# Output projection of a hybrid layer in seven block products, with weight sums kept in DRAM

## The chip, the cores and the metric

The kernel runs on one core of one Trainium2 chip. The metric is the device time of one execution in microseconds (us); the runs of the kernel before give 2102.1 us in the median.

## What is computed

One layer: a norm, one input projection, two token mixers side by side (HGRN2 and RG-LRU, 512 wide each), an output projection back to the residual stream, and a SwiGLU FFN. x has 2048 tokens of width 1024, all in float32.

```python
def reference(x, ...):
    h = x
    xn = rms_norm(h, mix_norm_w)
    proj = jnp.einsum('bsd,de->bse', xn, w_in)
    q, f_logit, i_v, g, lru_x, lru_gate = jnp.split(proj, ...)
    o_hg = hgrn2_mix(q, f_logit, i_v, g, lb, hg_norm_w)
    o_lru = rglru_mix(lru_x, lru_gate, ...)
    mixed = jnp.concatenate([o_hg, o_lru], axis=-1)
    h = h + jnp.einsum('bse,ed->bsd', mixed, w_out)
    hn = rms_norm(h, ffn_norm_w)
    gate, up = jnp.split(jnp.einsum('bsd,df->bsf', hn, w_gate_up), 2, axis=-1)
    h = h + jnp.einsum('bsf,fd->bsd', jax.nn.silu(gate) * up, w_down)
    return rms_norm(h, final_norm_w)
```

## The kernel before

**Numbers.** A float32 operand is split into a high part (a cast on ACT) and a low part (a subtraction on DVE), and each product of two operands is three matmuls: high by high, high by low, low by high. A matmul is 128x128 by 128x512.

**Stages.** The tokens come in two halves of 1024, and a half in two pieces c of 512 (four token tiles tt of 128). Mixing goes half by half. It makes the values (pv; `tok_wide` L589 in half 0, `tok_mm` L245 in half 1), then eight steps s of feature units (pa and pb, `feat_mm` L234), for HGRN2 where s is even and for the LRU where it is odd, with the state work in hooks between them, then the gate (pg). The gated HGRN2 output v is turned by PE (tp_o, four transposes a tile) and becomes, scaled and split, half of the operand mx; the LRU output y is the other half. The output projection (tiles poh, L1218 to L1246) has 2 pieces x 2 column halves n x 4 token tiles x 8 k x 3 = 384 matmuls a half. DVE adds x from PSUM into h (L1230), and h goes to DRAM. Behind it `scale_h` (L1202) makes the row factor of the FFN's norm and scales h, and `turn_h` (L1208) turns it (tp_hs) and stores it to hn_d. While half 0 is projected, `norm_steps` (L606) prepares the normed x of half 1 (xk, xn).

The FFN follows by halves: `ffn_up` in 22 quads, each in seven block products on sums of activation blocks (act_a to act_g) and of weights (wgu_a to wgu_g), 84 matmuls a quad; `down_quads` in seven products too; and, for six feature tiles of half 0, `down_plain` (L866) in plain products, one pass for c=0 and one for c=1. In the second of these the steps that load hn of half 1 and make its act operands are handed out one by one (`extra`): b_0 to b_3 are four blocks of hn.

**Weights.** `Stream` (L155) loads a weight tile of 512 KB into one of three raw buffers, casts the high part on ACT (L168) and subtracts on DVE (L169) into slots (whi, wlo), of which there are nine. `ahead` asks for tiles before their use.

**Order.** Within an engine instructions run in the order that the program's scheduler gave them, and wait there for their data; the loads and stores that SP issues also stand in one queue. Data wait in pools: 16 pages, 4 xin tiles, 14 blocks, 4 + 4 banks of PSUM. At the start `warm_up` (L518) runs zero matmuls while the first data come in (19 are written, and the trace has 38 records of them).

Of the kernel before, what the change touches and what calls it, by code (L numbers as in the profile page):

```python
# [18 lines left out]
NU = 4  # L19
# [18 lines left out]
def hybrid_layer(ctx: ExitStack, tc: tile.TileContext, x, x_t, norm_w, cols, w_in, gate_w, w_out, w_gu, w_down, out):  # L38
# [116 lines left out]
    class Stream:  # L155
# [3 lines left out]
        def load(self, line, i):  # L159
            src, nm = self.specs[i]  # L160
            raw = rawt("raw_" + nm)
            line(nc.sync.dma_start(out=raw, in_=src))
            return raw
# [23 lines left out]
    for half in range(2):  # L187
        for s in range(24):
            specs.append((w_in[s], f"in{half}_{s}"))
        for c in range(NC):  # L190
            for s in range(8):
                specs.append((w_out[s], f"o{half}_{c}_{s}"))
    ws = Stream(specs)

# [323 lines left out]
    def warm_up():  # L518
        z = late("warm")
        v.memset(z, 0.0)  # L520
        ps = aux("warm")
        for i in range(19):
            nc.tensor.matmul(ps[:, 0:P], lhsT=z[:, 0:P], rhs=z[:, P : 2 * P], start=True, stop=True)
# [10 lines left out]

    def row_factors(c, rows):
        rs = small.tile([P, 4], F32, tag="ss", name=f"ss_x0_{c}", bufs=8)
# [4 lines left out]
        v.scalar_tensor_tensor(out=rs, in0=sums[0], scalar=EPS, in1=sums[1], op0=ALU.add, op1=ALU.add)  # L541
        nc.gpsimd.tensor_tensor(out=rs, in0=rs, in1=mhalf, op=ALU.pow)
        return rs
# [17 lines left out]
    def row_spread(c, rs):  # L561
        nm = f"x0_{c}"
# [16 lines left out]

    def load_x(half, c, tt, nm):  # L580
        r0 = half * T + c * CW + tt * P
        xs = []
        for n in range(2):
            p = page(f"{nm}_{n}")
            nc.sync.dma_start(out=p, in_=x[r0 : r0 + P, n * CW : (n + 1) * CW])
            xs.append(p)
        return xs
# [18 lines left out]
    def norm_steps(half, c):  # L606
        o = half * T + c * CW
        box = {}

        def stat(tt):  # L610
            nm = f"x{half}_{c}_{tt}"
            if tt == 0:
                box["dg"], box["pbc"] = late(f"dg{half}_{c}"), aux(f"tpb{half}_{c}")
            dg, pbc = box["dg"], box["pbc"]
            rs = rstd_of(load_x(half, c, tt, nm), nm)
            ts = slice(tt * P, (tt + 1) * P)
            v.tensor_scalar(out=dg[:, ts], in0=ident, scalar1=rs, scalar2=None, op0=ALU.mult)
            nc.tensor.matmul(pbc[:, ts], lhsT=ones.broadcast_to([P, P]), rhs=dg[:, ts], start=True, stop=True)

        def apply(k):  # L620
            if k == 0:
                box["xn"] = act_tile(f"xn{half}_{c}")
            p = xin(f"xk{half}_{c}_{k}")
            nc.sync.dma_start(out=p, in_=x_t[k * P : (k + 1) * P, o : o + CW])
            v.scalar_tensor_tensor(
                out=p, in0=p, scalar=par[:, C_NW + k : C_NW + k + 1], in1=box["pbc"], op0=ALU.mult, op1=ALU.mult
# [3 lines left out]
        return box, [lambda tt=tt: stat(tt) for tt in range(TPC)], [lambda k=k: apply(k) for k in range(KT)]  # L630

# [442 lines left out]
    for half in range(2):  # L1079
# [12 lines left out]
        for c in range(NC):  # L1092
# [19 lines left out]
            for tt in range(TPC):  # L1112
                ps = tok_mm(wv, xt[c], tt, f"pv{half}_{c}_{tt}")
                nc.scalar.copy(out=vt[:, tt, :], in_=ps)
                if later:
                    later.pop(0)()
# [28 lines left out]
        for s in range(8):  # L1145
            i = s // 2
            ws.ahead(2)
# [24 lines left out]
        mixes = []  # L1172
        for c in range(NC):
# [9 lines left out]
            mx = act_tile(f"mx{half}_{c}")  # L1183
            for tt in range(TPC):
                transpose_in(mx, tt, 0, vts[c][:, tt, :], f"o{half}_{c}_{tt}", par[:, C_HN : C_HN + 1])
            for u in range(NU):
                split([part(mx, s, 4 + u) for s in range(2)], ys[c][:, u, :])
            mixes.append(mx)


        wffn = wvec(1, f"wffn{half}")
        if half == 0:
            boxes, steps = [], [[], []]
            for c in range(NC):
                nb, stats, applies = norm_steps(1, c)
                boxes.append(nb)
                steps[c] = stats + applies
        else:
            bops[0], steps, last = acts(hn_d[0], "0", False)
        hp = {}  # L1200

        def scale_h(half, g, wffn, hp):  # L1202
            rs = rstd_of(hp[g], f"hs{half}_{g}")
            for n in range(2):
                p = hp[g][n]
                v.scalar_tensor_tensor(out=p, in0=p, scalar=rs, in1=wffn[:, n * CW : (n + 1) * CW], op0=MUL, op1=MUL)

        def turn_h(half, g, hp):  # L1208
            nm = f"hs{half}_{g}"
            for n in range(2):  # L1210
                pt = transposed(g, n, hp[g][n], nm)
                q = late(f"ht{nm}_{n}")
                nc.scalar.copy(out=q.rearrange("p (k t) -> p k t", t=P), in_=pt)
                nc.sync.dma_start(
                    out=hn_d[half][n][:, :, g * P : (g + 1) * P].rearrange("k p t -> p k t"), in_=q.rearrange("p (k t) -> p k t", t=P)
                )

        later, turns = [], []  # L1218
        for c in range(NC):
            todo = len(steps[c])  # L1220
            for n in range(2):
                wo = ws.take(4)
                for tt in range(TPC):
                    g = c * TPC + tt
                    nm = f"h{half}_{g}_{n}"
# [126 lines left out]
```

## Time and profile before

| | us |
|---|---|
| runs (median; lowest to highest) | 2102.1; 2102.0 to 2103.07 |
| the profiled execution | 2103.02 |
| its span in the trace | 2101.3 |
| PE, DVE, ACT busy | 2086.6, 1516.6, 1001.5 |

PE is TensorE's matmul stream, PEld its weight loads, DVE VectorE, ACT ScalarE, POOL GpSimd, SP the queue that issues the transfers. A row of a timeline gives start, duration, engine, line, operation, out<-in, shapes and count, and in brackets the idle time before it and what ended it. A row of a window gives each engine's busy time in it with the number of instructions, then the granted clock of TensorE as a share (PEclk), the busy share of the DMA engines and GB/s. A row of what PE waited for gives us in total, times, and the longest. "x256 | 100.7, 393" in a group is count, busy us and mean ns.

### The profile page before, as it was taken

What the parts mean: (1) busy time and instruction counts of PE and PEld (TensorE: products, weight loads), DVE (VectorE), ACT (ScalarE), POOL (GpSimd) and SP (SyncE); (2) the same over time, 40 slices, a digit from 0 to 9 for tenths busy, and PEclk for the clock granted to TensorE, in tenths of its full rate; (3) what the DMA queues carried; (4) which work ended last, traced back from release to release, by engine and by line L of the source; (5) the groups of instructions that cost most, each with busy time, mean ns of one, the idle gap of its engine ahead of it and who ended that gap; (6) DMA issues with size and microseconds to landing.
All of it is one profiled execution on the core that took longest, in us unless ns stands there. A gap on an engine that the chain in (4) does not pass through costs nothing.

```text
span 2101.3 us, 26188 instructions
## 1 busy us (share of the span) xinstructions
PE 2086.6 (99%) x9682; PEld 1730.6 (82%) x9682; DVE 1516.6 (72%) x2467; ACT 1001.5 (48%) x1671; POOL 61.8 (3%) x111
## 2 busy tenths in 40 slices
PE   9999999999999999999999999999999999999998
PEld 8888888888888887888888888887888888888887
DVE  7778856626888558876676669778767676669787
ACT  7677765536777644433333344335333333344333
POOL 1000000100000000000000000000000000000000
PEclk9999999999999999999999999999999999999999
DMA  7111117831111176432232365345423232266424
GB/s 261 51 41 40 32 41 236 275 120 41 41 41 41 61 249 201 146 130 95 87 120 96 106 250 191 116 144 176 147 89 125 96 103 102 96 232 238 160 81 146
DMA packets 139712, 264.94 MB, mean 126 GB/s; under 512 B 11328, under 2 KB 27712, under 8 KB 139584
## 3 DMA queue, kind: packets, MB, share of 16 engines
q1 hardware_dynamic: 139440, 263.24, 37.3%
q8 instruction: 76, 1.25, 0.3%
q14 instruction: 52, 0.43, 0.1%
q10 hardware_dynamic: 144, 0.03, 0.0%
HBM read 200.04 MB, written 63.18 MB: 125 GB/s over the span
## 4 chain that ended last, share of the span: by engine, by line
PE 94%; DVE 3%; DMA 2%; issue 1%; ACT 0%; DVEq 0%; POOLq 0%; POOL 0%; SPq 0%; ACTq 0%
PE quad_e L756 11%; PE quad_g L756 11%; PE quad_a L756 11%; PE pda L1027 10%; PE pdb L1027 6%; PE quad_f L756 6%; PE pb L241 3%; PE pb L242 3%; PE pa L240 3%; PE pa L241 3%; PE pb L240 3%; PE pa L242 3%; PE poh L252 2%; PE poh L253 2%; PE poh L254 2%; PE pv L600 2%
## 5 line engine op out<-in xcount | busy, mean ns | idle before, releaser
L756 PE MATMUL quad_f<-act_f,wgu_f 128*128 128x512 f32 x528 | 127.4, 390 | 1.7 <-ACT wgu_c L212 1.5
L756 PE MATMUL quad_a<-act_a,wgu_a 128*128 128x512 f32 x528 | 127.6, 390 | 0.0
L756 PE MATMUL quad_g<-act_g,wgu_g 128*128 128x512 f32 x528 | 127.1, 390 | 0.0
L756 PE MATMUL quad_a<-act_b,wgu_b 128*128 128x512 f32 x528 | 127.1, 389 | 0.0
L756 PE MATMUL quad_g<-act_d,wgu_d 128*128 128x512 f32 x528 | 127.0, 390 | 0.0
L756 PE MATMUL quad_e<-act_e,wgu_e 128*128 128x512 f32 x528 | 127.0, 389 | 0.0
L756 PE MATMUL quad_e<-act_c,wgu_c 128*128 128x512 f32 x528 | 126.9, 389 | 0.0
L640 DVE TENSOR_TENSOR u<-u,quad_g 128x512 f32<-128x512 f32 x88 | 60.5, 688 | 80.0 <-PE quad_g L756 80.0
L756 PEld LDWEIGHTS quad_f<-act_f,wgu_f 128*128 128x128 f32 x528 | 99.1, 188 | 22.9 <-ACT act_g L212 1.9
L756 PEld LDWEIGHTS quad_g<-act_d,wgu_d 128*128 128x128 f32 x528 | 99.1, 188 | 20.9 <-DVE u L640 0.4
L756 PEld LDWEIGHTS quad_e<-act_c,wgu_c 128*128 128x128 f32 x528 | 99.1, 188 | 20.6
L756 PEld LDWEIGHTS quad_g<-act_g,wgu_g 128*128 128x128 f32 x528 | 99.0, 188 | 20.7 <-DVE wgu_g L213 0.3
L756 PEld LDWEIGHTS quad_e<-act_e,wgu_e 128*128 128x128 f32 x528 | 99.1, 188 | 20.5
L756 PEld LDWEIGHTS quad_a<-act_b,wgu_b 128*128 128x128 f32 x528 | 99.1, 188 | 20.5
L756 PEld LDWEIGHTS quad_a<-act_a,wgu_a 128*128 128x128 f32 x528 | 99.0, 188 | 20.4
L240 PE MATMUL pa<-xn,whi_in 128*128 128x512 f32 x256 | 101.1, 395 | 0.0
L241 PE MATMUL pb<-xn,wlo_in 128*128 128x512 f32 x256 | 100.7, 393 | 0.0
L242 PE MATMUL pb<-xn,whi_in 128*128 128x512 f32 x256 | 100.4, 392 | 0.0
L242 PE MATMUL pa<-xn,whi_in 128*128 128x512 f32 x256 | 100.4, 392 | 0.0
L241 PE MATMUL pa<-xn,wlo_in 128*128 128x512 f32 x256 | 100.4, 392 | 0.0
L240 PE MATMUL pb<-xn,whi_in 128*128 128x512 f32 x256 | 100.2, 392 | 0.0
L254 PE MATMUL poh<-whi_o,mx 128*128 128x512 f32 x256 | 99.2, 392 | 0.0
(337 smaller groups left out, 4902.3 us busy)
## 6 DMA issues: line engine op xcount, KB each, us to landing
raw<-in_w_gu SPq DMA_DIRECT2D x88, 512.0 KB, 3.9
raw_in<-in_w_in SPq DMA_DIRECT2D x47, 512.0 KB, 3.5
ao_p<-as SPq DMA_DIRECT2D x76, 256.0 KB, 2.7
raw_o<-in_w_out SPq DMA_DIRECT2D x32, 512.0 KB, 4.7
xk<-in_x_t SPq DMA_DIRECT2D x32, 256.0 KB, 5.1
x<-in_x SPq DMA_DIRECT2D x32, 256.0 KB, 5.7
xrh<-in_x SPq DMA_DIRECT2D x32, 256.0 KB, 3.5
h<-h SPq DMA_DIRECT2D x32, 256.0 KB, 3.6
```

Source lines behind the costliest of these rows:

```text
L240: nc.tensor.matmul(ps, lhsT=whi[:, ks], rhs=hi, start=(k == 0), stop=False)
L241: nc.tensor.matmul(ps, lhsT=wlo[:, ks], rhs=hi, start=False, stop=False)
L242: nc.tensor.matmul(ps, lhsT=whi[:, ks], rhs=lo, start=False, stop=(k == KT - 1))
L252: nc.tensor.matmul(ps, lhsT=hi, rhs=whi[:, ks], start=(k == 0), stop=False)
L253: nc.tensor.matmul(ps, lhsT=hi, rhs=wlo[:, ks], start=False, stop=False)
L254: nc.tensor.matmul(ps, lhsT=lo, rhs=whi[:, ks], start=False, stop=(k == KT - 1))
L600: ins = nc.tensor.matmul(banks[tt], lhsT=a, rhs=w, start=(k + i == 0), stop=(k == KT - 1 and i == 2))
L640: (e or v).tensor_tensor(out=out, in0=a, in1=b, op=op)
L756: nc.tensor.matmul(ps, lhsT=w[:, s, ks], rhs=x, start=first and k + n == 0, stop=k == 3 and n == 2, skip_group_check=not first)
L1027: nc.tensor.matmul(ps, lhsT=x, rhs=y, start=first and q + n == 0, stop=q == gr.n - 1 and n == 2, skip_group_check=not first)
```

## The change

The projection of a half is taken as one 2x2 product of blocks. The rows are c=0 and c=1, the inner dimension is hg (the turned HGRN2 output) and y, the columns are n=0 and n=1. Seven products replace eight: p1 = hg0 b11, p2 = y0 b21, and five on sums of operands, weights or both. They run in the order of OORDER; two groups of four banks, pox and poy, collect them, so that p6 is added on top of p1, p7 on top of that, and so on, and after each product DVE adds its bank into the right tile of the residual (res, L1303; 28 adds a half, where there were 16). Each product has 4 token tiles x 4 k x 3 = 48 matmuls, and two weight tiles of 512 KB from a stream of its own (wos).

The weight sums for p4, p5, p6 and p7 are made once, in half 0, at s = 1, 3, 5, 7 (`out_sums`): four loads of 256 KB into two of the raw buffers, four subtractions on DVE, four stores to DRAM (wo_p). Both halves load them from there.

The operand sums (`sum_`, L1224) are eight operations of 128x1024 on DVE a half; hg is copied out of PSUM by ACT alone, and splits are 128x1024 (two of them an operand).

h is stored to DRAM, and loaded again where it is scaled and turned (`h_steps`): for half 0 in the pv stage of half 1, for half 1 in the first `ffn_up`, one tile every 14 steps. `norm_steps` takes the squares of x in xin tiles, one power a piece c in place of one a tile, and DVE reads the row of factors from a copy in SBUF. `warm_up` has 11 zero matmuls. In `down_plain` of half 0 two empty steps stand after the first four of `extra`.

```diff
+    OORDER = ("p1", "p2", "p6", "p5", "p7", "p3", "p4")
+    t_d = {name: dram.tile([P, 4, CW], F32, name="wo_" + name) for name in ("p4", "p5", "p6", "p7")}
+    ospecs = []
+    for half in range(2):
+        for name in OORDER:
+            for kp in range(2):
+                at0 = {"p1": 0, "p2": 2, "p3": 6}.get(name)
+                ospecs.append((t_d[name][:, 2 * kp : 2 * kp + 2, :] if at0 is None else w_out[at0 + kp], f"o{half}_{name}_{kp}"))
+    wos = Stream(ospecs)
...
+    def out_sums(k):
+        kp, ks = k // 2, slice((k % 2) * CW, (k % 2 + 1) * CW)
+        r = [rawt(f"wt{u}_{k}") for u in range(2)]
+        for u in range(2):
+            for n in range(2):
+                nc.sync.dma_start(out=r[u][:, n * CW : (n + 1) * CW], in_=w_out[4 * n + 2 * u + kp][:, ks])
+        b11, b12, b21, b22 = (r[u][:, n * CW : (n + 1) * CW] for u in range(2) for n in range(2))
+        v.tensor_tensor(out=b11, in0=b12, in1=b11, op=ALU.subtract)
+        v.tensor_tensor(out=b12, in0=b22, in1=b12, op=ALU.subtract)
+        v.tensor_tensor(out=b22, in0=b22, in1=b11, op=ALU.subtract)
+        v.tensor_tensor(out=b21, in0=b21, in1=b22, op=ALU.subtract)
+        for name, p in (("p5", b11), ("p7", b12), ("p4", b21), ("p6", b22)):
+            nc.sync.dma_start(out=t_d[name][:, k, :], in_=p)
...
-        for i in range(19):
+        for i in range(11):
...
+            pbc = row_spread(c, box["rs"], "x1")
+            box["row"] = late(f"row1_{c}")
+            nc.scalar.copy(out=box["row"], in_=pbc)
...
+            if half == 0 and s % 2:
+                out_sums(i)
...
+        def operand(name, p):
+            op[name] = [block(f"mx_{LET[name]}{s}_{half}") for s in range(2)]
+            for j in (0, 2):
+                split([t[:, j : j + 2, :] for t in op[name]], p[:, j : j + 2, :])
+
+        def sum_(out, a, b, alu):
+            for j in (0, 2):
+                v.tensor_tensor(out=out[:, j : j + 2, :], in0=a[:, j : j + 2, :], in1=b[:, j : j + 2, :], op=alu)
+
...
+                tp = transposed(tt, 0, vts[c][:, tt, :], f"o{half}_{c}_{tt}")
+                nc.scalar.activation(
+                    out=t[:, :, tt * P : (tt + 1) * P], in_=tp, func=AF.Copy, scale=par[:, C_HN : C_HN + 1]
                 )
...
+        def prepare(name):
+            if name == "p6":
+                s1 = part_sums["s1"] = block(f"s1_{half}", F32)
+                s2 = part_sums["s2"] = block(f"s2_{half}", F32)
+                sum_(s1, hg[1], ys[1], ALU.add)
+                sum_(s2, s1, hg[0], ALU.subtract)
+                operand(name, s2)
+            elif name == "p5":
+                operand(name, part_sums["s1"])
+                sum_(hg[1], hg[0], hg[1], ALU.subtract)
+                sum_(ys[0], ys[0], part_sums["s2"], ALU.subtract)
+            elif name == "p7":
+                operand(name, hg[1])
+            elif name == "p3":
+                operand(name, ys[0])
+            elif name == "p4":
+                operand(name, ys[1])
...
+        to = dict(p1=(0, 0), p2=(0, 0), p6=(0, 1), p5=(1, 1), p7=(1, 1), p3=(0, 1), p4=(1, 0))
...
+        for i, name in enumerate(OORDER):
+            wo = wos.take(2)
+            if i < 6:
+                wos.ahead(2)
+                prepare(OORDER[i + 1])
+            if name in ("p2", "p5"):
+                banks_y = [aux(f"poy{name}_{tt}_{half}") for tt in range(TPC)]
+            banks = banks_y if name in ("p2", "p5", "p3") else banks_x
+            first = name in ("p1", "p2", "p5")
+            a = op.pop(name)
+            c, n = to[name]
+            if i in (1, 2, 5):
+                residual_in(*to[OORDER[i + 1]])
+            for tt in range(TPC):
+                tsl, ps = slice(tt * P, (tt + 1) * P), banks[tt]
+                for q in range(4):
+                    whi, wlo = (w[:, (q % 2) * CW : (q % 2 + 1) * CW] for w in wo[q // 2])
+                    ahi, alo = (z[:, q, tsl] for z in a)
+                    for m, (x_, y_) in enumerate(((ahi, whi), (ahi, wlo), (alo, whi))):
+                        nc.tensor.matmul(
+                            ps, lhsT=x_, rhs=y_, start=first and q + m == 0, stop=q == 3 and m == 2, skip_group_check=not first
+                        )
+                g = c * TPC + tt
+                p = res[g, n]
+                v.tensor_tensor(out=p, in0=p, in1=ps, op=ALU.add)
+                if name in ("p2", "p7", "p3", "p4"):
+                    nc.sync.dma_start(out=h_d[half][g][n], in_=p)
+                slot(4 * i + tt)
...
+        def h_steps(g, half=half, ffn_row=ffn_row):
+            ps = []
+            nm = f"hs{half}_{g}"
+
+            def scale():
+                if not ffn_row:
+                    ffn_row.append(wvec(1, f"wffn{half}"))
+                for n in range(2):
+                    p = page(f"{nm}_{n}")
+                    nc.sync.dma_start(out=p, in_=h_d[half][g][n])
+                    ps.append(p)
+                rs = rstd_of(ps, nm)
+                for n in range(2):
+                    v.scalar_tensor_tensor(
+                        out=ps[n], in0=ps[n], scalar=rs, in1=ffn_row[0][:, n * CW : (n + 1) * CW], op0=MUL, op1=MUL
+                    )
+
+            def turn():
...
+            later = [lambda i=i, p=pairs: (p[i][0]() if i < NTT else 0, p[i - 1][1]() if i else 0) for i in range(NTT + 1)]
+        else:
+            idle = [lambda: None]
+            later = idle * 14 + [f_ for p in pairs for f_ in idle + [p[0]] + idle * 2 + [p[1]] + idle * 9]
...
-            extra = steps + last
+            extra = [steps.pop(0) for _ in range(4)] + [lambda: None] * 2 + steps + last
```

**DVE in the output projection of half 0.** Before, around the first residual adds (poh is the projection's bank, ss_x and dg belong to the norm of half 1's x, mx is the operand):

```order
L169 TENSOR_TENSOR wlo_o_0_3_3002<-raw_o_0_3_2999,whi_o_0_3_3001 128x1024
L213 TENSOR_TENSOR mx_1_11_2942<-y_1_681,mx_1_01_2940 128x512 x4
L216 SCALAR_TENSOR_TENSOR mx_1_10_2941<-tp_o_1_3_0_2964,par,mx_1_00_2939 128x4x128
L1230 TENSOR_TENSOR h_0_0_3032<-xrh_0_0_3005,poh_0_0_3007 128x512
L1230 TENSOR_TENSOR h_1_0_3090<-xrh_1_0_3063,poh_1_0_3065 128x512
L206 SCALAR_TENSOR_TENSOR ss_x_0_0_3041<-ss_x_0_0_3041 128x1
L617 TENSOR_SCALAR dg_0_3035<-ident,ss_x_0_0_3041 128x128
L206 SCALAR_TENSOR_TENSOR ss_x_0_1_3054<-ss_x_0_1_3054 128x1
L1230 TENSOR_TENSOR h_2_0_3133<-xrh_2_0_3106,poh_2_0_3108 128x512
L617 TENSOR_SCALAR dg_0_3035<-ident,ss_x_0_1_3054 128x128
```

After, from the last add of p1 (pox) past the first low parts of p6's operand (mx_f); s_0_3172 is the sum s2, each sum being two such rows, and poyp_0_0 is p2's bank of the first token tile:

```order
L1303 TENSOR_TENSOR res_3_0_3048<-res_3_0_3048,pox_0_3053 128x512
L1224 TENSOR_TENSOR s_0_3172<-s_0_3171,hg_0_2839 128x1024
L1224 TENSOR_TENSOR hg_1_3017<-hg_0_2839,hg_1_3017 128x1024
L1303 TENSOR_TENSOR res_0_0_3042<-res_0_0_3042,poyp_0_0_3183 128x512
L1224 TENSOR_TENSOR y_0_676<-y_0_676,s_0_3172 128x1024
L170 TENSOR_TENSOR wlo_o_p_1_3168<-raw_o_p_1_3165,whi_o_p_1_3167 128x1024
L234 TENSOR_TENSOR mx_f_0_3178<-s_0_3172,mx_f_0_3177 128x1024
L1303 TENSOR_TENSOR res_1_0_3044<-res_1_0_3044,poyp_1_0_3184 128x512
```

Behind p1 and p2 now stand the operations on 128x1024 that make the sums, and mx_f comes behind them; before, the adds had row factors and weight low parts between them, and the operand was complete ahead of the first add.

**DVE where the plain down product goes from c=0 to c=1.** Before, the last rows up to the first add that frees a bank (hd from pd):

```order
L213 TENSOR_TENSOR act_d_1_11713<-b_2_1_11860,act_d_1_11712 128x512
L640 TENSOR_TENSOR b_3_1_11941<-b_3_1_11943,b_3_1_11941 128x512
L213 TENSOR_TENSOR ad_1_16_12004<-ad_1_16_12002,ad_1_16_12004 128x512
L213 TENSOR_TENSOR act_e_1_11703<-b_3_1_11940,act_e_1_11702 128x512
L213 TENSOR_TENSOR wlo_d_1_16_12010<-raw_d_1_16_12007,whi_d_1_16_12009 128x1024
L640 TENSOR_TENSOR b_3_1_11940<-b_3_1_11943,b_3_1_11940 128x512
L213 TENSOR_TENSOR act_g_1_11707<-b_3_1_11941,act_g_1_11706 128x512
L640 TENSOR_TENSOR b_3_1_11942<-b_3_1_11942,b_3_1_11940 128x512
L213 TENSOR_TENSOR act_f_1_11705<-b_3_1_11940,act_f_1_11704 128x512
L213 TENSOR_TENSOR ad_1_17_12015<-ad_1_17_12013,ad_1_17_12015 128x512
L640 TENSOR_TENSOR hd_0_0_10549<-hd_0_0_10549,pd_0_0_0_11635 128x512
```

After, the rows up to the same add (ad_1_16 and wlo_d_1_16 are the first operands of c=1):

```order
L234 TENSOR_TENSOR act_f_1_11703<-b_2_1_11856,act_f_1_11702 128x512
L234 TENSOR_TENSOR act_d_1_11711<-b_2_1_11858,act_d_1_11710 128x512
L234 TENSOR_TENSOR ad_1_16_11976<-ad_1_16_11974,ad_1_16_11976 128x512
L234 TENSOR_TENSOR wlo_d_1_16_11982<-raw_d_1_16_11979,whi_d_1_16_11981 128x1024
L234 TENSOR_TENSOR act_a_1_11699<-b_3_1_12084,act_a_1_11698 128x512
L234 TENSOR_TENSOR ad_1_17_11987<-ad_1_17_11985,ad_1_17_11987 128x512
L655 TENSOR_TENSOR hd_0_0_10547<-hd_0_0_10547,pd_0_0_0_11633 128x512
```

Of the work on the block b_3 the row with act_a is what still stands ahead of the add; the rows that make sums of b_3, and act_e, act_g and act_f of them, come behind it.

**SP in the feature steps of half 0.** Before, the loads of weight units stand alone:

```order
L162 DMA raw_in_6_682<-in_w_in 128x1024
L162 DMA raw_in_7_688<-in_w_in 128x1024
L162 DMA raw_in_8_903<-in_w_in 128x1024
L162 DMA raw_in_9_909<-in_w_in 128x1024
L162 DMA raw_in_10_1135<-in_w_in 128x1024
L162 DMA raw_in_11_1141<-in_w_in 128x1024
```

After (wt are the raw pieces of w_out, wo_p the sums in DRAM):

```order
L163 DMA raw_in_6_678<-in_w_in 128x1024
L163 DMA raw_in_7_684<-in_w_in 128x1024
L207 DMA wt_0_899<-in_w_out 128x512 x2
L214 DMA wo_p_101<-wt_0_899 128x512
L207 DMA wt_0_900<-in_w_out 128x512 x2
L163 DMA raw_in_8_913<-in_w_in 128x1024
L214 DMA wo_p_103<-wt_0_899 128x512
L214 DMA wo_p_102<-wt_0_900 128x512
L163 DMA raw_in_9_919<-in_w_in 128x1024
L214 DMA wo_p_100<-wt_0_900 128x512
L163 DMA raw_in_10_1145<-in_w_in 128x1024
```

Between two loads of weight units stand up to four loads or stores of the sums; a store stands in the queue until DVE has made what it stores.

More of the change, by code (lines that the diff above doesn't have):

```diff
@@ L161, in load @@
             raw = rawt("raw_" + nm)
-            line(nc.sync.dma_start(out=raw, in_=src))
+            to = raw if len(src.shape) == 2 else raw.rearrange("p (k w) -> p k w", w=CW)
+            line(nc.sync.dma_start(out=to, in_=src))
             return raw
@@ L559, in scaled, with row_spread @@
         return xw
[L561 to L562 removed]
+    def row_spread(c, rs, nm="x0"):
+        nm = f"{nm}_{c}"
         pbc, dg = aux("tpb" + nm), late("dg" + nm)
@@ L578, in normalised @@
         return xn
[L580 to L587, printed above, removed]
     def tok_wide(w4, xt, nm, between):
@@ L1114, in hybrid_layer @@
                 nc.scalar.copy(out=vt[:, tt, :], in_=ps)
-                if later:
-                    later.pop(0)()
+                later.pop(0)()
+        for f_ in later:
+            f_()
         if half == 0:
@@ L1182, in hybrid_layer @@
                 v.tensor_tensor(out=vts[c][:, tt, :], in0=vts[c][:, tt, :], in1=sg, op=ALU.mult)
-            mx = act_tile(f"mx{half}_{c}")
+                if c == 1:
+                    slot(tt - 4)
+            t = block(f"hg{half}_{c}", F32)
+            hg.append(t)
             for tt in range(TPC):
-                transpose_in(mx, tt, 0, vts[c][:, tt, :], f"o{half}_{c}_{tt}", par[:, C_HN : C_HN + 1])
-            for u in range(NU):
-                split([part(mx, s, 4 + u) for s in range(2)], ys[c][:, u, :])
@@ L1188, in hybrid_layer @@
[L1188 to L1215, printed above, removed]
-                )
[L1218 to L1225, printed above, removed]
-                    xr = xin("xr" + nm)
-                    nc.sync.dma_start(out=xr, in_=x[t0 + g * P : t0 + (g + 1) * P, n * CW : (n + 1) * CW])
-                    ps = tok_mm(wo, mixes[c], tt, "po" + nm)
-                    hp.setdefault(g, [None, None])[n] = page(nm)
-                    v.tensor_tensor(out=hp[g][n], in0=xr, in1=ps, op=ALU.add)
-                    nc.sync.dma_start(out=h_d[half][g][n], in_=hp[g][n])
-                    if n == 1:
-                        later.append(lambda half=half, g=g, wffn=wffn, hp=hp: scale_h(half, g, wffn, hp))
-                        turns.append(lambda half=half, g=g, hp=hp: turn_h(half, g, hp))
-                    if (n, c) != (1, 1):
-                        if len(turns) > 2 or (n == 0 and turns):
-                            turns.pop(0)()
-                        if later:
-                            later.pop(0)()
-                    i = n * TPC + tt + 1
-                    while steps[c] and todo - len(steps[c]) < -(-todo * i // 8):
-                        steps[c].pop(0)()
-                    if half == 1 and c == 1 and n == 1 and tt == 0:
@@ new lines, in hybrid_layer, with residual_in @@
+        res = {}
+        def residual_in(c, n):
+            for tt in range(TPC):
+                g = c * TPC + tt
+                res[g, n] = page(f"res{half}_{g}_{n}")
+                nc.sync.dma_start(out=res[g, n], in_=x[t0 + g * P : t0 + (g + 1) * P, n * CW : (n + 1) * CW])
+        to = dict(p1=(0, 0), p2=(0, 0), p6=(0, 1), p5=(1, 1), p7=(1, 1), p3=(0, 1), p4=(1, 0))
+        residual_in(0, 0)
+        banks_x = [bank(f"pox_{tt}_{half}") for tt in range(TPC)]
+        for i, name in enumerate(OORDER):
[11 more added lines that the diff above has]
+                residual_in(*to[OORDER[i + 1]])
+            for tt in range(TPC):
+                tsl, ps = slice(tt * P, (tt + 1) * P), banks[tt]
[6 more added lines that the diff above has]
+                        )
+                g = c * TPC + tt
+                p = res[g, n]
[3 more added lines that the diff above has]
+                slot(4 * i + tt)
+                if i == 6 and tt == 0:
+                    if half == 0:
+                        ws.ahead(4)
+                    else:
```

85 lines of the change are left out of this document (61 added, 24 removed).

## The prediction

> **What bounds the kernel now.** I read the page first, then what PE waited for, then windows, then the timeline at the few places where PE stands still.
>
> ```profile
> span 2101.3 us, 26188 instructions
> PE 2086.6 (99%) x9682; PEld 1730.6 (82%) x9682; DVE 1516.6 (72%) x2467; ACT 1001.5 (48%) x1671; POOL 61.8 (3%) x111
> PE 94%; DVE 3%; DMA 2%; issue 1%; ACT 0%; DVEq 0%; POOLq 0%; POOL 0%; SPq 0%; ACTq 0%
> ```
>
> PE is busy for 99% of the span, and the chain that ended last runs through it for 94%. So a matmul that goes is worth its full pace, unless its place is taken by a wait. What PE waits for now is short:
>
> ```profile
> PE pd L894 <- DVE hd L640: 2.2, 1, 2.2
> PE quad_f L756 <- ACT wgu_c L212: 1.5, 1, 1.5
> PE warm L523 <- DVE warm L520: 1.5, 1, 1.5
> PE pv L253 <- DVE wlo_in L169: 0.9, 1, 0.9
> PE pv L252 <- DVE h L1230: 0.5, 1, 0.5
> PE tp_hs L228 <- DVE h L1206: 0.4, 2, 0.2
> ```
>
> DVE decides what can go wrong. These windows (PE, PEld, DVE, ACT, POOL busy, PEclk, DMA share, GB/s) are the feature steps, the output projection of half 0 (318 to 411), that of half 1 (734 to 817), and the start of the FFN:
>
> ```profile
> 100.00:200.00 100.00, 100.00 (x509) 83.17 (x508) 75.91 (x174) 74.27 (x123) 6.30 (x10) 1.00 0.13 42
> 318.00:411.00 93.00, 93.00 (x438) 77.48 (x437) 59.23 (x95) 52.32 (x104) 8.67 (x14) 1.00 0.79 262
> 734.00:817.00 83.00, 83.00 (x384) 68.78 (x383) 54.25 (x79) 33.34 (x57) 2.18 (x4) 1.00 0.76 244
> 817.00:867.00 50.00, 47.88 (x221) 37.94 (x220) 41.41 (x71) 29.93 (x63) 3.96 (x4) 1.00 0.49 157
> ```
>
> **Fewer matmuls.**
>
> ```profile
> L252 PE MATMUL poh<-whi_o,mx x256: 387/389/479, 318.2 to 816.5; 128*128 128x512 f32 x128
> L253 PE MATMUL poh<-wlo_o,mx x256: 387/389/478, 318.5 to 816.7; 128*128 128x512 f32 x128
> L254 PE MATMUL poh<-whi_o,mx x256: 387/389/478, 318.7 to 817.0; 128*128 128x512 f32 x128
> ...
> 7.90 21.78 PE pv L600 x96
> ```
>
> The projection has 3 x 256 = 768 matmuls. Afterwards there are 2 halves x 7 products x 4 token tiles x 12 = 672, of the same shape. The last line is a piece of the chain: 96 matmuls of that shape in 21.78 us, 0.227 each. The listed 389 ns is latency; starts are 0.227 apart. So 96 fewer save **21.8 us**. Transposes stay equal in number.
>
> **Fewer zero matmuls at the start.**
>
> ```profile
> 1.52 6.38 PE L523 MATMUL warm<-warm 128*128 128x128 f32 x38 [1.52 <-DVE warm L520]
> 4.96 0.72 ACT L215 ACTIVATE xw<-xk,par 128x512 fp32r<-128x512 f32 x1 [2.44 <-DMA par<-in_cols]
> 5.80 0.43 DVE L555 CAST whi_in<-raw_in 128x512 fp32r<-128x512 f32 x1 [4.33 <-DMA raw_in<-in_w_in]
> 6.14 0.74 DVE L216 SCALAR_TENSOR_TENSOR xw<-xk,par,xw 128x512 fp32r<-128x512 f32 x1
> 7.65 0.71 PE L600 MATMUL pv<-whi_in,xw 128*128 128x512 f32 x2
> 8.01 1.41 DVE L216 SCALAR_TENSOR_TENSOR xw<-xk,par,xw 128x512 fp32r<-128x512 f32 x2
> ...
> 1.50:5.40 3.90, 3.88 (x18) 3.88 (x19) 0.00 (x0) 1.46 (x2) 3.37 (x15) 1.00 0.76 234
> ```
>
> There are 38 warm records, 18 of them by 5.40 us (0.216 apart) and 20 from there to 7.65 (0.11 apart). With 11 rather than 19 written, 22 records remain: 18 x 0.216 + 4 x 0.11 = 4.3, so they end near 5.9. The first pv then waits only for its cast weights (5.80 + 0.43 = 6.23) and starts near 6.25 instead of 7.65. The low part of xw (6.88) is wanted four matmuls later, at 7.2. That is **1.4 us**. [...] Here the pace doubled after some 3.9 us, and 4.3 us of warm-up with pv right behind should still do.
>
> **The stop in the plain down product.** The c=0 to c=1 boundary, on PE, then DVE up to it:
>
> ```profile
> 1428.36 0.39 PE L896 MATMUL pd<-whi_d,ad 128*128 128x512 f32 x1
> 1430.92 0.47 PE L894 MATMUL pd<-whi_d,ad 128*128 128x512 f32 x1 [2.18 <-DVE hd L640]
> ...
> 1432.92 0.63 PE L894 MATMUL pd<-whi_d,ad 128*128 128x512 f32 x1
> 1433.35 0.63 PE L895 MATMUL pd<-wlo_d,ad 128*128 128x512 f32 x1
> ...
> 1431.00:1436.00 5.00, 5.00 (x15) 0.66 0.69 234
> ```
> ```profile
> 1424.14 0.69 DVE L640 TENSOR_TENSOR b<-b,b 128x512 f32<-128x512 f32 x1
> 1424.74 0.69 DVE L213 TENSOR_TENSOR ad<-ad,ad 128x512 fp32r<-128x512 f32 x1
> 1425.35 0.69 DVE L213 TENSOR_TENSOR act_e<-b,act_e 128x512 fp32r<-128x512 f32 x1
> 1425.95 1.22 DVE L213 TENSOR_TENSOR wlo_d<-raw_d,whi_d 128x1024 fp32r<-128x1024 f32 x1
> 1427.08 0.69 DVE L640 TENSOR_TENSOR b<-b,b 128x512 f32<-128x512 f32 x1
> ...
> 1430.09 1.29 DVE L640 TENSOR_TENSOR hd<-hd,pd 128x512 f32<-128x512 f32 x2
> ```
>
> PE waits 2.18 us for the hd add that frees a bank. The add waits for nothing but its place in DVE's queue: DVE runs back to back, one operation of 128x512 every 0.60 us and one of 128x1024 every 1.13. After the stop the clock column falls to 0.66, and eight matmuls start 0.43 apart instead of 0.227: 1.6 more, 3.8 in all. In the order of before, ten operations on the last activation block (b_3 and what is made of it) stand ahead of that add; now one does (act_a). Nine fewer at 0.60 are 5.4 us, more than 2.2, so the stop goes: **3.8 us**. The moved work falls into c=1 (six steps of 24 matmuls, 33 us of PE); what it makes is wanted only in the FFN of half 1. [...]
>
> **The operand sums and splits.** Here DVE could now be late for p6, the first product on sums.
>
> ```profile
> 317.98 0.44 PE tp_o L228 x4
> ```
>
> From the order of half 0: PE has 96 matmuls (p1, p2: 21.8) and four groups of transposes (0.44 each), 23.5 us, up to p6's first matmul. DVE cannot finish s1 before the last tp_o is copied: that comes after 31 matmuls (7.0), its own 0.44 and a copy on ACT like that of xw (0.72), so 8.2 us in. Then ten operations of 128x1024 and three adds stand up to and with p6's first low parts: 8.2 + 10 x 1.14 + 3 x 0.6 = 21.4, two before PE comes. The second low parts stand four large and two small operations further on, at 27.2, and PE, which goes around its four banks, wants them about 13 matmuls into p6, at 26.5. By spacing the stall is near 0.7; by the rows' durations (1.22, 0.69) it is nearly 3 more, about 4; at best none. I take 0.7 a half, **1.4 us lost**: the spacing is what a busy DVE shows.
>
> In all of half 0's projection DVE has 40 operations of 128x1024, 46 adds or subtractions of 128x512 and 20 scaled ones (0.66, the second of the two from 8.01): 88 us with the small ones. But 22 of them serve c=1 of the next pv; 65 stand against PE's 76 (336 x 0.227). So after p6 DVE gains on PE again.
>
> In half 1, DVE loses the 16 scalings of h (10.6 us) and two wlo (2.3), and gets eight sums (9.1), 12 more adds (7.2) and larger splits (14 x 1.14 against 8 x 0.66 + 8 x 0.60, 5.9): 9.3 more. From 734 to 867 it had 95.7 busy of 133; now 105 of 122, 86%. The last of act_f is queued some 15 us past the projection's end, and PE wants it some 25 past it. I count nothing, with 0 and the 10.6 of the first rival as bounds.
>
> **Counted at nothing.** The weight sums of half 0: 16 subtractions (11 us of DVE where it is 76% busy), 16 loads and 16 stores of 256 KB where the DMA share is 0.13. A store that waits for DVE holds the raw_in loads behind it on SP's queue, by a load, four subtractions and a store, about 10 us (3.6 + 4 x 0.69 + 3.6); a step has 96 matmuls of pa and pb (six groups like the one below over 16 steps), so at least 21.8 us, and its weights are asked for a step ahead. The h tiles, reloaded, scaled and turned later: 16 loads a half on SP's queue; one of them stands behind its own store and ahead of p7's weights, which are wanted over 20 us later.
>
> ```profile
> L241 PE MATMUL pb<-xn,wlo_in 128*128 128x512 f32 x256 | 100.7, 393 | 0.0
> ...
> raw_o<-in_w_out SPq DMA_DIRECT2D x32, 512.0 KB, 4.7
> h<-h SPq DMA_DIRECT2D x32, 256.0 KB, 3.6
> ```
>
> Two weight loads a product at 4.7 us, one after the other, stay under a product's 10.9; the 32 loads of x for the residual are as many as before. The POOL powers only move. hg made by ACT alone takes 16 scaled operations off DVE. [...] The four smaller waits in the list (3.3 without pd's and warm's) I leave as they are.
>
> **The sum.** The profiled execution took 2103.02 (span 2101.3 and 1.7 around it), 0.9 above the median of the runs. 2103.0 - 21.8 - 1.4 - 3.8 + 1.4 = **2077.4**; the 0.9 is left to the range.
>
> **Rivals.**
> - DVE becomes the bound at the FFN's start. 41.4 of those 50 us were busy; with the 9.3 it is full, and PE waits up to 9, and 1.6 at half clock: 2077.4 + 10.6 = 2088.0. For it: PE already stops there for 1.5. Against: some 10 us of slack by the order. 20%.
> - The boundary change doesn't do what it says, since act_a, still ahead of the add, waits for its load: 2077.4 + 3.8 = 2081.2. 15%.
> - The small waits go too, their order being new: 2077.4 - 3.3 = 2074.1. 10%.
> - The clock starts late: half pace for 3.8 us, as from 1431.7, loses 1.8: 2079.2. Against: pv follows the zero matmuls at once. 3%. [...]
> - Slower: DVE sets the pace of all 14 products, because products, splits and next norm are queued in one order. By spacing its 88 us make 12.6 a product against PE's 10.9, 24 us lost, 2101 (the stall at p6 is part of it): the gain is gone. By durations, 95.5 us make 13.6, 38 lost: **2115**. It decides from 10.9 + 25.6 / 14 = 12.7 us a product. Against: a quarter of that work has until pv. 7%, of which 4% beyond the bound.
>
> **Chances.** The forecast itself has 45%, within 2073 to 2081. To leave out no more than 2 in 10 the range goes from 2071 (small waits gone, no stall at p6, the median's 0.9) to 2089 (the first rival with a little more at p6). Within 0.2%, 4.2 us, a measurement cannot tell a change of this kernel from none. Faster 0.93, same 0.03, slower 0.04.
>
> **What would show it.** 672 matmuls under the projection; pv first at 6.25; no idle near the c=0 to c=1 boundary of the plain down product, and PEclk 1.00 there; PE's wait for mx_f at p6 of about 0.7 us a half; no wait of quad_f or quad_g over 2 us in the 30 us after half 1's projection. Wrong it would be if PE waits for wlo_o_p product after product, or for act_f and act_d.

## The result and the profile after

The changed kernel takes 2072.93 us in the median (2072.74 to 2073.64, four runs), the kernel before beside it 2102.05 (2100.79 to 2103.07): a ratio of 0.9862, with a 95% interval of 0.9845 to 0.9879. That is 29.1 us, where 25.6 were forecast from the profiled execution. The profiled execution of the changed kernel took 2073.64, with a span of 2071.6, so the two spans to compare are 29.7 apart.

The page of the changed kernel, in the same lines as before:

```profile
span 2071.6 us, 26049 instructions
PE 2059.0 (99%) x9570; PEld 1709.1 (83%) x9570; DVE 1555.6 (75%) x2509; ACT 1014.7 (49%) x1681; POOL 73.7 (4%) x105
PE 96%; ACT 1%; DVE 1%; DMA 1%; issue 0%; POOL 0%; DVEq 0%; POOLq 0%; ACTq 0%; SPq 0%
```

PE has 112 records fewer: 96 of the projection and 16 zero matmuls. DVE has 39 us more to do. PE still carries the chain. What it waits for (us in total, times, longest) is another list altogether:

```profile
PE warm L544 <- DVE warm L541: 1.5, 1, 1.5
PE tpbx L591 <- DVE dgx L590: 1.4, 1, 1.4
PE pox L1298 <- DVE mx_f L234: 1.2, 1, 1.2
PE pg L273 <- ACT sg L295: 0.8, 1, 0.8
PE quad_a L771 <- ACT e L808: 0.3, 1, 0.3
```

The waits of pd, quad_f, pv and tp_hs are gone; three of the four new ones (tpbx, mx_f, sg) lie in half 0, around its projection. The start, the first projection matmul, and the boundary in the plain down product, in the timeline of the changed kernel:

```profile
1.52 4.50 PE L544 MATMUL warm<-warm 128*128 128x128 f32 x22 [1.52 <-DVE warm L541]
6.14 1.62 PE L615 MATMUL pv<-whi_in,xw 128*128 128x512 f32 x6
...
342.97 0.73 PE L1298 MATMUL pox<-whi_o_p,mx_f 128*128 128x512 f32 x2 [1.20 <-DVE mx_f L234]
354.04 0.49 PE L591 MATMUL tpbx<-dgx,ones 128*128 128x128 f32 x2 [1.39 <-DVE dgx L590]
...
1402.95 0.39 PE L911 MATMUL pd<-whi_d,ad 128*128 128x512 f32 x1
1403.17 0.39 PE L909 MATMUL pd<-whi_d,ad 128*128 128x512 f32 x1
1403.40 0.39 PE L910 MATMUL pd<-wlo_d,ad 128*128 128x512 f32 x1
```

At the boundary the matmuls follow each other every 0.227 us. To see where the time went, the starts of the first matmul of each stage are taken from both traces, and the lengths are their differences (ffn_up ends with its last quad, and the last row at the last matmul):

| stage on PE | before | after | difference |
|---|---|---|---|
| zero matmuls, up to the first pv | 6.13 | 4.62 | -1.5 |
| pv of half 0 | 45.47 | 45.48 | 0.0 |
| features and gate of half 0 | 265.04 | 264.45 | -0.6 |
| projection of half 0 | 93.30 | 82.59 | -10.7 |
| pv, features and gate of half 1 | 314.34 | 315.99 | +1.7 |
| projection of half 1 | 91.39 | 76.76 | -14.6 |
| ffn_up of half 0 | 426.67 | 427.04 | +0.4 |
| down of half 0 | 221.43 | 217.37 | -4.1 |
| FFN of half 1 | 628.10 | 628.10 | 0.0 |

The rows add up to 29.4 of the 29.7 us; the other 0.3 lie behind the last matmul. The 48 matmuls that each projection lost are 10.9 us. Half 1's projection lost 3.7 more: the 32 transposes that turned h in it (tp_hs, 3.0 us of PE) now stand elsewhere, and the rest is many small gaps. pv of half 1 and ffn_up took these turnings in and got longer by less than they cost, because waits that stood there (pv 0.9 and 0.5, quad_f 1.5 and 0.2, tp_hs 0.4) went.

DVE around half 1's projection and the FFN's start (PE, PEld, DVE, ACT, POOL busy, PEclk, DMA share, GB/s):

```profile
714.00:791.00 77.00, 77.00 (x348) 63.85 (x346) 70.66 (x92) 37.82 (x51) 0.00 (x0) 1.00 0.75 257
791.00:841.00 50.00, 49.68 (x219) 40.72 (x218) 43.30 (x71) 22.42 (x42) 0.22 (x1) 1.00 0.34 118
```

DVE is busy for 92% and 87% of these windows, and PE waits in them for 0.3 us.

### The profile page after: what moved, and what is told of

It reads as the page before. It is cut to its first block, busy times and chain, and to the rows that moved or that the text cites. A ratio compares the mean times of both kernels' runs of the same rounds, so it can differ in the third digit from the quotient of the medians.

```text
span 2071.6 us, 26049 instructions
## 1 busy us (share of the span) xinstructions
PE 2059.0 (99%) x9570; PEld 1709.1 (83%) x9570; DVE 1555.6 (75%) x2509; ACT 1014.7 (49%) x1681; POOL 73.7 (4%) x105
## 4 chain that ended last, share of the span: by engine, by line
PE 96%; ACT 1%; DVE 1%; DMA 1%; issue 0%; POOL 0%; DVEq 0%; POOLq 0%; ACTq 0%; SPq 0%
PE quad_e L771 12%; PE quad_g L771 12%; PE quad_a L771 12%; PE pda L1042 10%; PE pdb L1042 7%; PE quad_f L771 6%; PE pox L1298 4%; PE pa L261 3%; PE pb L262 3%; PE pa L263 3%; PE pb L263 3%; PE pa L262 3%; PE pb L261 3%; PE poyp L1298 3%; PE pv L615 2%; PE pd L910 1%
```

## The experiments

The times are medians of 4 to 15 runs unless said otherwise. The kernel before, run beside them on four chips, had medians of 2101.0, 2099.9, 2100.4 and 2102.6, with single runs up to 5.4 us away; the changed kernel's runs spread by 0.9. So the medians are compared with the changed kernel's 2072.93, and what a part costs is read from the lengths of stages in the profiles.

**The zero matmuls.** In the changed kernel:

```diff
-        for i in range(11):
+        for i in range(19):
```

> The changed kernel with 19 zero matmuls instead of 11. Theory (first pv waits for the zero matmuls only): first pv at 7.65 us again instead of 6.14, all else equal, so 1.5 us over the changed kernel, 27.6 below the kernel before. Rival (the shorter warm-up costs clock elsewhere, or the gain is taken back by a later wait): within 0.4 us of the changed kernel, 29.1 below before.

2074.35 us, 1.4 over the changed kernel. The first pv starts at 7.82 instead of 6.14, and no other stage differs by over 0.5. The theory holds. The other way, five zero matmuls, was run on the kernel hg_first, which is told of below (2070.15):

```diff
-        for i in range(11):
+        for i in range(5):
```

> The kernel hg_first with 5 zero matmuls instead of 11 (10 records, over at about 3.7 us, then some 2.4 us of idle before the first pv). Theory (the pace doubles after about 3.9 us of work, so a shorter warm-up is paid in real matmuls at half pace): pv starts no earlier than 6.0, its first 8 to 16 matmuls come 0.43 apart, 1.7 to 3.4 us over hg_first. Rival (the clock is at full pace by 5.5 us whatever ran before): within 0.4 us of hg_first.

2073.21 us, 3.1 over hg_first. PE's timeline of it:

```profile
1.52 2.50 PE L544 MATMUL warm<-warm 128*128 128x128 f32 x10 [1.52 <-DVE warm L541]
6.20 3.55 PE L615 MATMUL pv<-whi_in,xw 128*128 128x512 f32 x8 [2.18 <-DVE whi_in L579]
9.59 1.08 PE L615 MATMUL pv<-wlo_in,xw 128*128 128x512 f32 x4
```

Eight matmuls take 3.4 us, 0.42 each, before the pace of 0.227 comes: 1.6 us lost, as the theory has it. Another 1.3 us of the difference lies between pv and the projection of half 0 (265.8 against 264.5 us). There the scheduler gave PE's instructions another order than in hg_first, so these 1.3 are not shown to be a price of the warm-up. With 11, the zero matmuls of hg_first go on to 6.0, and pv follows there with no slow matmul. So it is in nine of the ten profiles of kernels with 11 zero matmuls. In the tenth (hsteps_early, below) the full pace came only at 7.4 us, two of pv's matmuls started 0.56 and 0.42 apart, and pv is 0.5 us longer (45.96 against 45.48). So the late clock, which the prediction had as a rival at 3%, does happen with 11, and cost 0.5 us there.

**The plain down product.** In the changed kernel, without the two empty steps:

```diff
-            extra = [steps.pop(0) for _ in range(4)] + [lambda: None] * 2 + steps + last
+            extra = steps + last
```

> The changed kernel, with the steps that prepare half 1's activations handed out in the plain down product as before (no two empty steps). Theory (what stands ahead of the first hd add in DVE's queue makes the stop): the stop of about 2.2 us and the eight matmuls at half pace come back, 3.8 to 4.1 us over the changed kernel, 25 to 25.3 below before. Rival (the stop went because all that comes before it shifted): within 0.4 us of the changed kernel, 29.1 below before.

2073.78 us, 0.9 over the changed kernel, and the stage is 217.83 us long against 217.37. The stop did not come back, although ten operations on b_3 stand ahead of the first hd add again, as in the kernel before. So the rows ahead of the add did not make the stop by themselves. Both small edits alone, on the kernel before:

```diff
-        for i in range(19):
+        for i in range(11):
...
-            extra = steps + last
+            extra = [steps.pop(0) for _ in range(4)] + [lambda: None] * 2 + steps + last
```

> The kernel before, with 11 zero matmuls and the two empty steps, and nothing else changed. Theory (both terms stand on their own): 1.5 + 4.1 = 5.6 us below before. Rival (the stop's end needs the rest of the change): 1.5 us below before. Third (both terms are made by the shift): 0 to 0.5 us below.

2096.41 us (eleven runs) against 2101.01 for the kernel before beside it, 4.6 less; the spans of the profiles are 5.8 apart. The down stage is 217.37 us long, 4.1 less than in the first profile of before, and the first pv starts at 6.39. So there the empty steps do end the stop. pv of half 1 lost its waits too (47.2 us against 49.1), though PE's order there is the same, and a wait of 1.2 for an h add came at the FFN's start: small waits went and came here where the kernel was the same. A second profile of the kernel before:

> The kernel before, unchanged, for a second profile. Theory (the stop at the c=0 to c=1 boundary is made by a late load of hn, which pushes DVE's queue, so that its length changes from run to run): the wait of pd for hd differs from 2.2 us by over 0.5, and with it the landing of the load that act_a waits for. Rival (it is made by the order of DVE's rows alone): 2.2 us again, within 0.2.

One run, 2100.91 us. PE and ACT at the same place, from the first profile of before and then from this one:

```profile
1417.53 0.62 ACT L212 CAST act_a<-b 128x512 fp32r<-128x512 f32 x1 [3.36 <-DMA b<-hn]
```

```profile
1416.87 0.62 ACT L212 CAST act_a<-b 128x512 fp32r<-128x512 f32 x1 [3.36 <-DMA b<-hn]
...
1430.26 0.47 PE L894 MATMUL pd<-whi_d,ad 128*128 128x512 f32 x1 [2.13 <-DVE hd L640]
...
1431.00:1436.00 5.00, 5.00 (x23) 3.90 (x22) 5.00 (x9) 3.38 (x9) 0.54 (x1) 1.00 0.50 178
```

The stop is there again, 2.13 us, and so is the wait of act_a's cast for the load of hn, 3.36 us. In these two executions its length is the same, as the rival said. But this time no matmul behind it ran at half pace: 23 in the five microseconds, PEclk 1.00, where there were 15 and 0.66. The stage is 219.93 us long against 221.43. So the half clock is no fixed part of the stop's price; it is 2.6 or 4.1 us. In no_spacing the same cast (1390.34) waits 1.92 for its load, and counted from the first pd of each kernel it comes 2.1 us earlier:

```profile
1390.34 0.62 ACT L233 CAST act_a<-b 128x512 fp32r<-128x512 f32 x1 [1.92 <-DMA b<-hn]
```

19.45 us after the first pd (1370.89) there, 21.59 (1395.94) in before. From that cast on DVE runs back to back up to the hd add in both. These are act_a's low part and that add, in before and then in no_spacing:

```profile
1418.18 0.69 DVE L213 TENSOR_TENSOR act_a<-b,act_a 128x512 fp32r<-128x512 f32 x1 [2.33 <-ACT act_a L212]
...
1430.09 1.29 DVE L640 TENSOR_TENSOR hd<-hd,pd 128x512 f32<-128x512 f32 x2
```

```profile
1390.99 0.69 DVE L234 TENSOR_TENSOR act_a<-b,act_a 128x512 fp32r<-128x512 f32 x1 [0.89 <-ACT act_a L233]
...
1402.90 1.28 DVE L655 TENSOR_TENSOR hd<-hd,pd 128x512 f32<-128x512 f32 x2
```

The add starts 11.91 us behind act_a's low part in both, so the 2.1 us by which the cast is later in before are the 2.1 us by which the add is late, and PE stops for 2.18. By these rows the stop is a load that lands late, carried to the add by a full queue: the empty steps shorten the queue, and in the changed kernel the load lands earlier anyway. No run moved the load alone. Why it lands earlier was not found: it is issued 0.7 us sooner, and takes 1.4 less.

**What the projection of half 0 waits for.** The loads and squares of half 1's x four slots later:

```diff
-                    at_slot(-4 + 4 * c + j, f_)
+                    at_slot(4 * c + j, f_)
```

> The changed kernel with the squares and loads of half 1's x moved from the last four gate tiles and first four projection tiles (slots -4 to 3) to the first eight projection tiles (slots 0 to 7). Theory A (in half 0 PE's waits for sg 0.8 and mx_f 1.2 come from these loads and squares, which hold the loads and casts of p6's weight sums and so the last copy of hg on ACT): these two go, 1.5 to 2.5 us below the changed kernel, 30.6 to 31.6 below before. Theory B (p6 waits because DVE's chain of sums is too long, as the prediction had it): mx_f's wait stays at 1.2, and the time within 0.8 of the changed kernel.

2072.97 us, no different in the median. The edit moved nothing: in the trace every engine's instructions stand in the order of the changed kernel, and the squares start where they did (the first, in the changed kernel and then in this one):

```profile
300.51 0.63 ACT L632 ACTIVATE x<-x 128x512 f32<-128x512 f32 x1 [1.62 <-DMA x<-in_x]
```

```profile
300.58 0.64 ACT L632 ACTIVATE x<-x 128x512 f32<-128x512 f32 x1 [1.54 <-DMA x<-in_x]
```

So this run tests neither theory; it is the changed kernel once more. PE's waits for sg (0.8) and tpbx (1.4) are as they were, and the one for mx_f is 0.3 in place of 1.2. That wait changes by itself: it is 0.7 in warm19, 1.5 in no_spacing, 1.1 in spread_later, 1.8 in hsteps_early and 0.3 in sums_twice, none of which touches this place. ACT in the changed kernel shows what stands ahead of it:

```profile
328.01 1.05 ACT L169 CAST whi_o_p<-raw_o_p 128x1024 fp32r<-128x1024 f32 x1 [2.18 <-DMA raw_o_p<-wo_p]
328.96 0.68 ACT L1243 ACTIVATE hg<-tp_o,par 128x512 f32<-128x512 f32 x1
```

The last copy of hg, which the sums need, stands behind the cast of p6's first weight tile, and that cast waits for its load (2.18 us here, 1.52 where mx_f's wait was 0.3). Putting the copy first:

```diff
-                    at_slot(8 + c, spread)
+                    at_slot(8 + 6 * c, spread)
...
+                if i == 1:
+                    with tc.issue_after(copied.ins):
+                        wos.ahead(2)
                 wos.ahead(2)
```

The first of these lines was run alone before, as spread_later; copied is the last copy of hg.

> The changed kernel with the row factors of c=1 (dgx on DVE, tpbx on PE) six slots later in half 0's projection (slot 15 in place of 9). Theory (PE's wait of 1.4 us at tpbx is its place in PE's queue: DVE makes dgx behind weights and splits that PE needs only later): the wait goes, 1.4 us below the changed kernel, span near 2069.5. Rival (DVE is short of time there, so the wait moves to the next product): within 0.4 us of it.

2071.30 us, 1.6 under the changed kernel. The wait at tpbx is gone, mx_f's stays at 1.1, and the projection of half 0 is 80.50 us long instead of 82.59. The wait was a place in PE's queue, as the theory has it.

> The kernel spread_later, and on ACT the cast of p6's first weight sum tile behind the last copy of hg instead of ahead of it; nothing else moves. Theory (in half 0 the sums start late because that copy stands behind a cast that waits 2.2 us for its load, and not because the chain of sums is too long): the copy comes 2 to 3 us earlier and PE's wait for mx_f (1.1 to 1.2) goes; 1.1 us below spread_later, 30 below before. Rival (the chain of sums itself is too long, or the weight is then late): a wait of 0.7 or more stays at p6.

2070.15 us (2069.78 to 2070.30) against 2100.37 for the kernel before beside it: 0.9856, 0.9841 to 0.9871, 2.8 under the changed kernel and the best of all. What PE still waits for, and ACT at that place:

```profile
PE warm L544 <- DVE warm L541: 1.5, 1, 1.5
PE pg L273 <- ACT sg L295: 0.8, 1, 0.8
PE quad_a L771 <- ACT e L808: 0.3, 1, 0.3
```

```profile
324.59 1.06 ACT L169 CAST whi_o_p<-raw_o_p 128x1024 fp32r<-128x1024 f32 x1
325.53 0.71 ACT L1243 ACTIVATE hg<-tp_o,par 128x512 f32<-128x512 f32 x1
327.79 1.05 ACT L169 CAST whi_o_p<-raw_o_p 128x1024 fp32r<-128x1024 f32 x1 [1.56 <-DMA raw_o_p<-wo_p]
```

The copy comes at 325.53 instead of 328.96, the cast behind it waits for its load (1.56), and PE's wait at p6 is gone, here and in warm5, which is built on this kernel. The chain of sums is short enough. What stays is 0.8 us at sg, which no run took away; by the trace of the changed kernel ACT runs there back to back, and four sg come behind other activations and table loads (1.28 us each, five from 283 to 296.8). The other way to give the chain time, p5 ahead of p6 (what prepares the operands is put in the same order):

```diff
-    OORDER = ("p1", "p2", "p6", "p5", "p7", "p3", "p4")
+    OORDER = ("p1", "p2", "p5", "p6", "p7", "p3", "p4")
...
```

> The changed kernel with p5 ahead of p6 in both halves: p5 needs s1 alone, and s2 and the differences are made a product later. Theory A (p6's operand is late by its chain and by the last copy of hg, which on ACT stands behind a weight cast that waits for its load): p5's operand is five DVE operations nearer, so mx's wait of 1.2 us in half 0 goes; 0.7 to 1.5 us below the changed kernel. Theory B (p5 right behind p2 takes p2's banks and waits for p2's adds): a wait of poyp for res adds, 0.5 to 2 us in each half, within 0.5 below to 3 above.

2078.14 us, 5.2 over. mx's wait is gone, as theory A says, but p5 waits for banks. That is theory B's place, with more behind it than p2's adds. PE's waits there:

```profile
PE poyp L1298 <- ACT row L639: 3.2, 1, 3.2
PE poyp L1298 <- ACT whi_o_p L169: 2.1, 1, 2.1
...
PE poyp L1298 <- DVE res L1303: 0.6, 1, 0.6
```

p5 follows p2 on the same four banks, and tpbx takes one of them too: in half 0 p5 waits 3.2 us for the copy that frees it, and twelve matmuls behind that stop start 0.43 apart (PEclk 0.50 from 348.5 to 354), 2.4 us more. In half 1 it waits 2.1 for a weight cast. p2's add, the only wait that theory B named, costs 0.6.

**How much DVE can take.** One more operation behind each of the 28 adds of a half:

```diff
                 v.tensor_tensor(out=p, in0=p, in1=ps, op=ALU.add)
+                v.tensor_tensor(out=p, in0=p, in1=p, op=ALU.max)
```

> The changed kernel with one more DVE operation of 128x512 behind each of the 28 residual adds a half (maximum of the tile with itself), 0.60 us each, 16.8 a half. Theory (DVE is short only up to p6 and gains on PE afterwards, about 10 us by p4): eight of them stand ahead of mx_f, so PE's wait there grows by up to 4.8 a half; 4 to 10 us over the changed kernel. Rival (DVE sets the pace of all products): 25 to 34 over. Third (DVE has slack everywhere): under 1 over.

2090.83 us, 17.9 over (15.7 between the profiled executions). The projection of half 0 is 3.8 us longer, with 5.1 of waiting for mx_f (theory); that of half 1 is 0.1 longer (76.88 against 76.76), and ffn_up 11.8 (438.87 against 427.04). The largest waits, and the FFN's start:

```profile
PE pox L1298 <- DVE mx_f L234: 5.1, 2, 2.8
PE quad_g L771 <- DVE wgu_g L234: 3.6, 1, 3.6
PE quad_f L771 <- DVE wgu_f L234: 3.6, 1, 3.6
...
795.00:845.00 50.00, 41.23 (x167) 32.12 (x166) 48.20 (x81) 23.67 (x42) 0.00 (x0) 0.90 0.41 141
```

None of the three forecasts fits the whole. DVE doesn't set the pace of the products: 16.8 us more of it cost half 1's projection nothing. The work is put off to the FFN's start, where DVE then is full (48.2 of 50). Of the 11.8 us, 8.5 are waits (PE stands still for 8.8 us there, and for 0.3 in the changed kernel). Most of the rest is half pace behind the stops of 3.6 us: PEclk is 0.68, 0.50 and 0.80 in the five-microsecond windows from 805 to 820. So of 16.8 us of work 8.5 could not be hidden, and some 8 us of DVE's time were free there, by this estimate.

**The turning of h at the FFN's start.** Half 1's h steps packed into the first 40 slots:

```diff
-            later = idle * 14 + [f_ for p in pairs for f_ in idle + [p[0]] + idle * 2 + [p[1]] + idle * 9]
+            later = [f_ for p in pairs for f_ in idle + [p[0]] + idle * 2 + [p[1]]]
```

> The changed kernel with half 1's reload, scaling and turning of h packed into the first 40 of the 154 slots of half 0's ffn_up (now spread over 126, from the 16th on). Theory (the small waits at the FFN's start in the kernel before, 2.1 us, went because the scalings and turns were taken out of DVE's and PE's queues there): waits of 1 to 3 us come back near the FFN's start. Rival (they went because the order at that place fell out otherwise): within 0.4 us of the changed kernel.

2076.15 us, 3.2 over, and ffn_up is 430.43 us long, 3.4 more. PE waits for hs (0.7, one of the turnings) and 0.9 at quad_a, where the changed kernel waits 0.3 in all. Waits of the size that the theory gives come back, so these steps cost time where DVE is crowded. They are other waits than those of the kernel before, though: quad_f's 1.5 for wgu_c did not return. That taking the steps out is what ended that one is likely by this, and not shown.

**The weight sums twice.**

```diff
                 out_sums(i)
+                out_sums(i)
```

> The changed kernel with each step of out_sums done twice (16 more loads and stores of 256 KB, 16 more DVE subtractions in half 0's feature steps; the same values are stored again). Theory (they lie wholly beside PE's work, which waits there for nothing): within 0.5 us of the changed kernel. Rival (SP's queue and the raw buffers held by them cost something that the stage lengths hide): 1 to 10 us over it, seen as waits of pa or pb for weights.

2079.14 us, 6.2 over. Features and gate of half 0 are 270.70 us long against 264.45. PE's waits there are for DVE and ACT, not for weights:

```profile
PE pg L273 <- ACT sg L295: 2.1, 1, 2.1
...
PE pk L379 <- DVE lg L366: 1.0, 2, 0.8
PE po L428 <- DVE sct L399: 0.8, 2, 0.5
```

So the first set is free (the stage is 0.6 us shorter than without it in the kernel before), and a second is not: the rival is right on the size, but PE waits for results of DVE and ACT, and not for weights. What makes DVE late is not separated by this run: it has 16 more operations in its queue, and it also stands idle for 6.0 us for the loads of the sums' own pieces (wt), where that is 2.0 in the changed kernel.

## Why the prediction was right, point by point

- **96 matmuls, 21.8 us.** The records count 112 fewer with the 16 zero ones, and p1's and p2's pace is the one that was used. Not tested by itself; the stage lengths agree with it within what else moved.
- **The zero matmuls, 1.4.** Measured 1.5 in the profile and 1.4 by warm19. The clock was not late here, with some luck: "4.3 us of warm-up with pv right behind should still do" rests on one start, and over the thirteen profiles without a pause the full pace came 3.1 to 5.9 us behind the first matmul. In one of the ten with 11 zero matmuls it came too late.
- **The stop in the plain down product, 3.8.** Its size in the profile was 4.1, but the mechanism was half wrong. "The add waits for nothing but its place in DVE's queue" left out what had made the queue late: a cast on ACT that waits for a load of hn, 12 us earlier. By no_spacing the stop goes in the changed kernel without the empty steps (0.5 us of stage length is their share), and by before_two the empty steps alone end it in the kernel before. And 1.6 of the 3.8 was a half clock that the second profile of before does not have: there the prediction rested on one row of one execution. Of six stops of 1.8 to 2.2 us in the profiles, two were followed by half pace (last section).
- **p6, 0.7 a half lost.** 1.2 in half 0 (0.3 to 1.8 over seven profiles) and nothing in half 1. The sum came near by chance: the chain of sums was reckoned from a last copy of hg that is done 8.2 us in, and that copy began at 12.9 (328.96, with the first matmul at 316.06), behind a cast that waits for its load. With the copy moved (hg_first) it is done 10.2 us in, still later than reckoned, and the wait is gone: so the chain behind it was reckoned too long, and two errors offset each other. The bound above is off too: by the durations (fourteen large and five small operations, 0.08 and 0.09 longer each) the prediction's own sum gives a stall of 2.3, not "about 4".
- **"The four smaller waits in the list (3.3 without pd's and warm's) I leave as they are."** This step failed, and it is most of the 3.8 us by which the sum stands above the profiled execution (2077.4 against 2073.64): all four went. The rival that had them go gave 2074.1 and 10%, and the measured 2072.93 is nearest to it. That the one at the FFN's start came from the scalings and turnings of h is likely by hsteps_early; those of pv also went in before_two, where only a shift can have done it. In return came 1.4 at tpbx and 0.8 at sg, which the prediction didn't have; they are about made up by small gains elsewhere (features of half 0 0.6, p6 of half 1 0.7, the down stage and the end 0.3 each), whose causes were not followed.
- **DVE at the FFN's start.** The rival was not met, with DVE busy for 87% of those 50 us. It stood some 8 us away, by dve_extra, where the prediction said some 10.
- **DVE as the pace of all products.** Not so: with 16.8 us more on DVE, half 1's projection kept its length, and half 0's grew by 3.8.
- **The weight sums at nothing.** Right, with less cover than was argued: a second set costs 6.2.

## What to carry to other kernels

A wait in a profile that is put down to a queue has a beginning: follow the queue back to the last place where its engine stood idle, since what ended that idle time (here a load of hn that ACT waited 3.36 us for) is what made the queue late. When a change takes work out of a crowded stretch, ask of each small wait there whose queue it stood in, and do not carry it over by habit. A small edit is read only when the trace shows that it moved what it was meant to move: one of these moved nothing, and its 0.9 us at mx_f were the spread of the same kernel. Of work that hides now, doubling it tells how much cover is left, which the busy share alone (75% to 92% on DVE here) does not.

## What was not expected of the hardware

An idle stretch of 2.18 us on PE was followed by half pace in one profile of the kernel before (8 matmuls 0.43 apart, PEclk 0.66), and one of 2.13 at the same place, in another execution, by none (PEclk 1.00). All fourteen profiles together, past the start, show how far this goes:

| PE stands still for | followed by half pace |
|---|---|
| 1.1 to 1.7 us, twelve stops | none |
| 1.8 to 2.2 us, six stops | 1.78 (hsteps_early) and 2.18 (before), but not 2.11 (sums_twice), 2.13 (before_again), 2.15 (p5_first), 2.23 (dve_extra) |
| 2.8 to 3.6 us, four stops | all: 2.84, 3.58 with 1.27 behind it, 3.63 (dve_extra), 3.23 (p5_first) |

Each time it was some six to twelve matmuls, 1.4 to 2.4 us. At the start PE reached its full pace between 4.6 and 7.4 us in the thirteen profiles that began at 1.52 and went on without a long pause, and at 9.6 in the one that stood still from 4.0 to 6.2 (warm5). The column PEclk says 1.00 for these slow starts too (warm5, 6.0 to 13.0), so there the pace has to be read from the distance of the matmuls. Why one stop is followed by half pace and its like is not, and why the start varies by 2.8 us, no run here shows.
